# The short convolution's taps as wide GpSimd instructions, and its input turned by VectorE

## The chip, the cores and the metric

One core of a Trainium2 chip runs the whole kernel in one launch. The metric is device time in microseconds (us). The engines are TensorE (PE in the profile, its weight loads PEld), VectorE (DVE), ScalarE (ACT), GpSimd (POOL) and SyncE (SP, which here only issues DMAs).

## What is computed

A decoder trunk of two layers on 256 tokens of 1024 channels, float32. Each layer is a half-weight SwiGLU, a mixer with three branches (gated short convolution, mLSTM, top-k sparse attention) merged by sigmoid gates, a second half-weight SwiGLU, and a gated input embedding; a last RMSNorm follows. The change touches one branch of the mixer:

```python
def short_conv_mixer(b_gate, c_gate, xc, conv_w, w_out):
    u = c_gate * xc                                   # (256, 512)
    up = jnp.pad(u, ((0, 0), (CONV_W - 1, 0), (0, 0)))  # CONV_W = 3
    y = up[:, 0:S] * conv_w[0]
    for j in range(1, CONV_W):
        y = y + up[:, j:j + S] * conv_w[j]
    return (b_gate * y) @ w_out
```

## The kernel before, in words

**Matmuls.** Every product of activations with weights is made of three matmuls (`mm3`, lines 205 to 207): high part by high part, high by low, low by high. A weight comes by DMA into `raw`; ScalarE copies it into the high part `wh` (line 157), VectorE subtracts to get the low part `wl` (line 158: two inputs in SBUF, one output). A *unit* is four blocks of 128 rows by 512 columns: two such pairs of 128x1024. Four units of `wh` and `wl` fit (`wpool`, 4 buffers). `project` (line 222) runs the units of one projection; for each it emits the two splits, then 12 matmuls for each half of the tokens, and after each 12 it calls `tick`.

**Order.** Work that isn't a projection stands in generators in two queues. `tick` takes one step from the head of each queue, so this work is emitted in slices between groups of 12 matmuls; `drain` ticks until a named generator is done. `queues[0]` holds the attention (`dsa`), `queues[1]` in this order the mLSTM gates, the turns of its queries and keys, its heads, then `conv`, `conv_gate`, `mlstm_out(0)`, `mlstm_out(1)`. The emitted order is a priority: a planner that runs when the kernel is built puts each engine's instructions in an order by its own reckoning of when each is ready, and an engine then runs them strictly in that order. So an instruction emitted late can stand early on an engine that would be idle.

**The convolution.** `ccn` (tokens on partitions, 2 x 512 channels) is the product of the gate and the input (lines 756 and 759). `conv` (line 762) turns it so that channels lie on partitions: `pe_turn` (line 289) makes, in two steps of one per half of the tokens, four TensorE transposes of 128x128 into one `tp` tile in PSUM (line 294) and one ScalarE copy to SBUF (line 295). Then, for each of four blocks of 128 channels in a step of its own, VectorE makes the three taps: one tensor-scalar (line 767) and two scalar-tensor-tensor on shifted columns (line 770). `conv_gate` turns the second gate `cbn` on TensorE (line 785), multiplies it into `cv` from PSUM on VectorE (line 786) in two steps, and splits the product into high and low parts.

**What else stands there.** In the same stretch the attention's softmax of the second half of the queries goes: scores on TensorE (line 575), scaling and mask on VectorE (line 577), maximum (line 585), exponentials on ScalarE (line 588), division by the sum on VectorE (line 592), four heads at a time, and then eight transposes of the result into two `tp` tiles on TensorE (line 603). There are two `tp` tiles in all. `mlstm_out` turns the mLSTM output with `turn` (line 283): sixteen VectorE instructions that turn 32x32 blocks, four in a step. Then ScalarE and VectorE scale and split it (lines 804 and 805). The output projections follow: attention, convolution, mLSTM, each behind its gate projection.

Of the kernel before, what the change touches and what calls it, by code (L numbers as in the profile page):

```python
# [13 lines left out]
ALU = mybir.AluOpType  # L14
AX = mybir.AxisListType

P = 128
T = 256
# [19 lines left out]
def trunk_kernel(  # L38
# [7 lines left out]
    nc = tc.nc  # L46
# [11 lines left out]
    def nm(s):  # L58
        uid[0] += 1
        return f"{s}_{uid[0]}"  # L60
# [4 lines left out]
    def tps(shape=(P, 4, P)):  # L65
        return psum.tile(list(shape), F32, name=nm("tp"), tag="tp", bufs=2)
# [11 lines left out]
    def mid(shape, dt=F32):  # L78
        return spool.tile(list(shape), dt, name=nm("mid"), tag="mid", bufs=7)
# [32 lines left out]
    G_FFN1, G_MIX, G_FFN2, G_PLE, G_ML, G_CONV = 0, 16, 32, 48, 64, 80  # L112
    gains = cpool.tile([P, 104], F32, name="gains")
# [165 lines left out]
    def turn(dst, src):  # L279

        for i in range(4):
            for j in range(4):
                nc.vector.transpose(  # L283
                    dst[32 * j:32 * j + 32].rearrange("p f (b i t) -> p b f i t", b=NB, i=4)[:, :, :, i, :],
                    src[32 * i:32 * i + 32].rearrange("p b (f j a) -> p b f j a", j=4, a=32)[:, :, :, j, :])
            if i < 3:
                yield

    def pe_turn(dst, src):

        for b in range(NB):
            tp = tps()
            for f in range(4):
                nc.tensor.transpose(tp[:, f, :], src[:, b, f * P:(f + 1) * P], ident)  # L294
            nc.scalar.activation(dst[:, :, b * P:(b + 1) * P], tp, AF.Copy)
            yield
# [176 lines left out]
    def mixer(l, xs, next_norm):  # L473
# [279 lines left out]
        ccn = mid([P, NB, 512])  # L753
# [6 lines left out]
        cv = mid([P, 4, T])  # L760

        def conv():
            uT = mid([P, 4, T])
            yield from pe_turn(uT, ccn)
            for j in range(4):
                g = [gains[:, G_CONV + 12 * l + 4 * i + j:G_CONV + 12 * l + 4 * i + j + 1] for i in range(3)]
                nc.vector.tensor_scalar(cv[:, j, :], uT[:, j, :], g[2], None, op0=ALU.mult)
                for i in (1, 0):
                    s = 2 - i
                    nc.vector.scalar_tensor_tensor(cv[:, j, s:], uT[:, j, :T - s], g[i], cv[:, j, s:],  # L770
                                                   op0=ALU.mult, op1=ALU.add)
                yield

        queues[1].append(conv())
        cbn = mid([P, NB, 512])
        ps = proj(0)
# [276 lines left out]
```

## Time and profile before

| | |
|---|---|
| median of three runs | 1363.99 us (1363.87 to 1364.86) |
| the profiled execution's own time | 1362.95 us |
| span of its trace | 1361.2 us |
| PE busy | 1350.5 us (99%) |
| DVE busy | 1100.4 us (81%) |
| ACT busy | 727.3 us (53%) |
| POOL busy | 24.9 us (2%) |
| granted TensorE clock, mean | 0.999 |

The span is that of the instructions; the time also holds what lies around them (1.75 us here). Busy matmuls are pipelined: a matmul of 512 columns is shown with 390 ns, while the next one starts some 230 ns after it. In rows of the timeline, columns are start, duration (of the whole row, where several are merged), engine, line, operation, output and inputs, shape, count, and in brackets the idle time before it with what ended it.

### The profile page before, as it was taken

How to read it: one execution, taken by the hardware profiler on the slowest of the kernel's cores; microseconds unless marked ns; L12 is line 12 of the kernel's file. 1: busy time of each engine (PE TensorE's matmuls, PEld its weight loads, DVE VectorE, ACT ScalarE, POOL GpSimd, SP SyncE). 2: the span in 40 equal slices, each digit the busy share in tenths (PEclk: the TensorE clock that was granted, in tenths of full speed). 3: DMA queues.
4: the chain of work that ended last, by engine and by line, in shares of the span. 5: the costliest groups of instructions: out<-in, count | busy, mean ns of one | idle time of the engine just before them, and what ended most of it. 6: DMA issues, size and time to landing. Idle time of an engine off the chain costs nothing.

```text
span 1361.2 us, 17307 instructions
## 1 busy us (share of the span) xinstructions
PE 1350.5 (99%) x6156; PEld 1108.9 (81%) x6156; DVE 1100.4 (81%) x2067; ACT 727.3 (53%) x1137; POOL 24.9 (2%) x42
## 2 busy tenths in 40 slices
PE   9999999999999999999999999999999999999997
PEld 7888888877888888888888888888778888888886
DVE  7988879859957888897788888797697588988976
ACT  6544466666544554454664444666665446444554
POOL 0000000000000000000000000000000000000000
PEclk9999999999999999999999999999999999999999
DMA  7755556643665656476546666655437655565661
GB/s 246 252 199 186 186 179 196 191 124 124 202 204 173 197 191 204 135 249 201 171 155 201 193 203 200 187 180 177 124 118 241 198 168 177 182 196 183 218 203 43
DMA packets 163426, 250.33 MB, mean 184 GB/s; under 512 B 7964, under 2 KB 101260, under 8 KB 163340
## 3 DMA queue, kind: packets, MB, share of 16 engines
q1 hardware_dynamic: 162700, 247.91, 56.9%
q8 instruction: 48, 0.79, 0.2%
q0 software_dynamic: 352, 1.06, 0.2%
q14 instruction: 38, 0.31, 0.1%
q10 hardware_dynamic: 288, 0.26, 0.1%
HBM read 248.14 MB, written 1.06 MB: 183 GB/s over the span
## 4 chain that ended last, share of the span: by engine, by line
PE 95%; DVE 2%; issue 1%; ACT 1%; DMA 0%; SPq 0%; POOLq 0%; POOL 0%; ACTq 0%
PE acc L205 24%; PE acc L207 24%; PE acc L206 24%; PE acc L434 18%; PE tp L264 1%; DVE mid L283 1%; DVE wl L158 1%; PE acc L724 1%; PE acc L575 1%; PE acc L511 0%; PE tp L294 0%; PE tp L603 0%; DMA x<-in_x_dram 0%; PE acc L707 0%; PE acc L537 0%
## 5 line engine op out<-in xcount | busy, mean ns | idle before, releaser
L158 DVE TENSOR_TENSOR wl<-raw,wh 128x1024 fp32r<-128x1024 f32 (+1 forms) x472 | 554.2, 1209 | 95.0 <-ACT wh L157 93.1
L157 ACT ACTIVATE wh<-raw 128x1024 fp32r<-128x1024 f32 (+1 forms) x472 | 475.6, 1044 | 229.1 <-issue 92.5
L205 PE MATMUL acc<-wh,xh 128*128 128x512 f32 (+1 forms) x1384 | 543.4, 393 | 0.8 <-ACT wh L157 0.8
L206 PE MATMUL acc<-wl,xh 128*128 128x512 f32 (+1 forms) x1384 | 537.5, 389 | 0.8 <-DVE wl L158 0.8
L207 PE MATMUL acc<-wh,xl 128*128 128x512 f32 (+1 forms) x1384 | 537.5, 389 | 0.0
L207 PEld LDWEIGHTS acc<-wh,xl 128*128 128x128 f32 x1384 | 260.0, 188 | 53.0
L205 PEld LDWEIGHTS acc<-wh,xh 128*128 128x128 f32 x1384 | 260.2, 188 | 52.6 <-ACT wh L157 1.2
L206 PEld LDWEIGHTS acc<-wl,xh 128*128 128x128 f32 x1384 | 260.3, 188 | 52.2 <-DVE wl L158 1.2
L283 DVE STREAM_TRANSPOSE half<-half 32x128 f32<-32x128 f32 x672 | 203.6, 303 | 12.7 <-DMA half<-in_p_dram 2.7
L434 PE MATMUL acc<-wh,mid 128*128 128x512 f32 x704 | 198.4, 392 | 0.0
L434 PEld LDWEIGHTS acc<-wh,mid 128*128 128x128 f32 x704 | 131.2, 188 | 27.5 <-ACT mid L267 0.9
L434 PE MATMUL acc<-wl,mid 128*128 128x512 f32 x352 | 108.6, 390 | 0.0
L157 ACT ACTIVATE mid<-half 128x512 fp32r<-128x512 f32 x42 | 26.6, 633 | 145.9 <-DVE half L283 145.9
L381 DVE SCALAR_TENSOR_TENSOR half<-acc,r,half 128x256 f32<-128x256 f32 x88 | 41.8, 480 | 64.8 <-ACT half L380 64.8
L380 ACT ACTIVATE half<-acc,r 128x256 f32<-128x256 f32 x88 | 41.2, 472 | 95.7 <-PE acc L207 95.6
L434 PEld LDWEIGHTS acc<-wl,mid 128*128 128x128 f32 x352 | 66.1, 188 | 13.8
L206 PE MATMUL acc<-wl,big 128*128 128x512 f32 x128 | 50.0, 391 | 0.0
L205 PE MATMUL acc<-wh,big 128*128 128x512 f32 x128 | 49.9, 390 | 0.0
L207 PE MATMUL acc<-wh,big 128*128 128x512 f32 x128 | 49.8, 389 | 0.0
L274 ACT ACTIVATE xh<-tp,gains 128x128 fp32r<-128x128 f32 x120 | 39.3, 362 | 12.4 <-DVE xl L275 8.6
L275 DVE SCALAR_TENSOR_TENSOR xl<-tp,gains,xh 128x128 fp32r<-128x128 f32 x120 | 38.3, 345 | 7.5 <-ACT xh L274 6.6
L283 DVE STREAM_TRANSPOSE mid<-big 32x256 f32<-32x256 f32 x96 | 41.8, 436 | 1.3
(189 smaller groups left out, 732.5 us busy)
## 6 DMA issues: line engine op xcount, KB each, us to landing
raw<-in_ffn_w_gu_dram SPq DMA_DIRECT2D x172, 512.0 KB, 5.1
raw<-in_w_in_dram SPq DMA_DIRECT2D x128, 512.0 KB, 4.3
raw<-in_ffn_w_down_dram SPq DMA_DIRECT2D x88, 512.0 KB, 4.7
raw<-in_mlstm_w_out_dram SPq DMA_DIRECT2D x16, 512.0 KB, 3.9
raw<-in_w_o_dram SPq DMA_DIRECT2D x16, 512.0 KB, 4.1
raw<-in_ple_w_gate_dram SPq DMA_DIRECT2D x16, 512.0 KB, 4.9
raw<-in_attn_w_out_dram SPq DMA_DIRECT2D x8, 512.0 KB, 3.9
raw<-in_conv_w_out_dram SPq DMA_DIRECT2D x8, 512.0 KB, 4.8
```

What stands on the lines that cost most here:

```text
L157: made = nc.scalar.activation(hi, v, AF.Copy).ins
L158: nc.vector.tensor_tensor(lo, v, hi.bitcast(F32), op=ALU.subtract)
L205: nc.tensor.matmul(ps, ah, wh, start=start, stop=False)
L206: nc.tensor.matmul(ps, ah, wl, start=False, stop=False)
L207: nc.tensor.matmul(ps, al, wh, start=False, stop=stop)
L264: turned[0] = nc.tensor.transpose(tp[:, j, :], src_of(k0 + j), ident).ins
L274: his.append(nc.scalar.activation(hi, tp[:, j:j + 1, :], AF.Copy, scale=g).ins)
L275: nc.vector.scalar_tensor_tensor(lo, tp[:, j:j + 1, :], g, hi.bitcast(F32), op0=ALU.mult, op1=ALU.subtract)
L283: nc.vector.transpose(dst[32 * j:32 * j + 32].rearrange("p f (b i t) -> p b f i t", b=NB, i=4)[:, :, :, i, :], src[32 * i:32 * i + 32].rea ...
L380: nc.scalar.activation(s[:, b, :], ps[b][:, :FCH], AF.Silu, scale=r)
L381: nc.vector.scalar_tensor_tensor(s[:, b, :], ps[b][:, FCH:], r, s[:, b, :], op0=ALU.mult, op1=ALU.mult)
L434: nc.tensor.matmul(dn[b][n], a, w[:, n * 512:(n + 1) * 512], start=c == 0 and f == 0 and a is ah and w is wh, stop=c == NFC - 1 and f == 1 ...
```

## The change

`conv` turns its input with `turn` (sixteen VectorE instructions in four steps) and makes the taps as five GpSimd instructions over all 4 x 256 columns: three products with a per-channel gain spread along the tokens, two additions of a shifted product. The two products that are added need a tile each (`mid`, a ring of seven buffers). The generator has five steps; before it had six.

```diff
         def conv():
             uT = mid([P, 4, T])
-            yield from pe_turn(uT, ccn)
-            for j in range(4):
-                g = [gains[:, G_CONV + 12 * l + 4 * i + j:G_CONV + 12 * l + 4 * i + j + 1] for i in range(3)]
-                nc.vector.tensor_scalar(cv[:, j, :], uT[:, j, :], g[2], None, op0=ALU.mult)
-                for i in (1, 0):
-                    s = 2 - i
-                    nc.vector.scalar_tensor_tensor(cv[:, j, s:], uT[:, j, :T - s], g[i], cv[:, j, s:],
-                                                   op0=ALU.mult, op1=ALU.add)
-                yield
+            yield from turn(uT, ccn)
+            yield
+            g = [gains[:, G_CONV + 12 * l + 4 * i:G_CONV + 12 * l + 4 * i + 4, None].to_broadcast([P, 4, T])
+                 for i in range(3)]
+            nc.gpsimd.tensor_tensor(cv, uT, g[2], op=ALU.mult)
+            for i in (1, 0):
+                s = 2 - i
+                part = mid([P, 4, T])
+                nc.gpsimd.tensor_tensor(part, uT, g[i], op=ALU.mult)
+                nc.gpsimd.tensor_tensor(cv[:, :, s:], part[:, :, :T - s], cv[:, :, s:], op=ALU.add)
+            yield
```

## Rows read from the trace of the kernel before

**Rows 1.** The page: busy time of each engine, and the chain of work that ended last, by engine.
```profile
PE 1350.5 (99%) x6156; PEld 1108.9 (81%) x6156; DVE 1100.4 (81%) x2067; ACT 727.3 (53%) x1137; POOL 24.9 (2%) x42
...
PE 95%; DVE 2%; issue 1%; ACT 1%; DMA 0%; SPq 0%; POOLq 0%; POOL 0%; ACTq 0%
```

**Rows 2.** The waits of TensorE in the whole span: who waited for whom, us in total, times, longest.
```profile
PE acc L205 <- ACT wh L157: 0.8, 1, 0.8
PE acc L206 <- DVE wl L158: 0.8, 1, 0.8
```

**Rows 3.** Busy time of the engines in two stretches of the second layer (us from the span's start): stretch and its length, then PE, PEld, DVE, ACT, POOL with counts, granted clock, DMA share, GB/s.
```profile
967.20:985.00 17.80, 17.80 (x88) 13.16 (x87) 10.76 (x19) 11.11 (x28) 1.67 (x1) 1.00 0.39 119
985.00:999.00 14.00, 14.00 (x68) 11.17 (x66) 13.74 (x29) 10.01 (x19) 0.00 (x0) 1.00 0.25 71
```

**Rows 4.** The timeline of TensorE around one of the convolution's groups of four transposes, second layer.
```profile
977.58 0.39 PE L207 MATMUL acc<-wh,xl 128*128 128x512 f32 x1
977.90 1.14 PE L575 MATMUL acc<-akT,mid 64*128 64x256 f32 x8
978.97 0.66 PE L294 MATMUL tp<-ident,mid 128*128 128x128 f32 x4
979.38 0.48 PE L205 MATMUL acc<-wh,xh 128*128 128x512 f32 x1
```

**Rows 5.** Groups of instructions by line and shape over the whole span (count, then busy us and mean ns of one). Of line 294 and line 295 a third is the convolution's; the rest turns the mLSTM's queries and keys.
```profile
L283 DVE STREAM_TRANSPOSE mid<-big 32x256 f32<-32x256 f32 x96 | 41.8, 436 | 1.3
...
L294 PE MATMUL tp<-ident,mid 128*128 128x128 f32 x48 | 7.4, 277 | 0.0
L295 ACT ACTIVATE mid<-tp 128x512 f32<-128x512 f32 x12 | 7.0, 586 | 4.7 <-PE tp L294 4.7
...
L770 DVE SCALAR_TENSOR_TENSOR mid<-mid,gains,mid 128x255 f32<-128x255 f32 x8 | 3.8, 478 | 0.0
...
L767 DVE TENSOR_SCALAR mid<-mid,gains 128x256 f32<-128x256 f32 x8 | 2.8, 350 | 0.0
```

**Rows 6.** The timeline of VectorE, second layer: softmax, taps and the first split behind them.
```profile
985.42 1.13 DVE L592 TENSOR_SCALAR big<-big,sm 128x256 f32<-128x256 f32 x4
...
986.73 1.22 DVE L585 TENSOR_REDUCE mx<-big 128x4 f32<-128x1024 f32 x1
...
988.32 0.35 DVE L767 TENSOR_SCALAR mid<-mid,gains 128x256 f32<-128x256 f32 x1
...
989.37 0.35 DVE L767 TENSOR_SCALAR mid<-mid,gains 128x256 f32<-128x256 f32 x1
...
991.15 1.13 DVE L592 TENSOR_SCALAR big<-big,sm 128x256 f32<-128x256 f32 x4
...
992.59 1.21 DVE L158 TENSOR_TENSOR wl<-raw,wh 128x1024 fp32r<-128x1024 f32 x1
```

**Rows 7.** The timeline of ScalarE in the same stretch: the first of the second four exponentials, and the weight copies behind the last of them.
```profile
988.45 0.51 ACT L588 ACTIVATE big<-big,mx 128x256 f32<-128x256 f32 x1 [1.35 <-DVE mx L586]
...
990.44 1.99 ACT L157 ACTIVATE wh<-raw 128x1024 fp32r<-128x1024 f32 x2
```

**Rows 8.** The timeline of TensorE, second layer: the transposes of the softmax and the products behind them.
```profile
994.80 1.03 PE L603 MATMUL tp<-ident,big 128*128 128x128 f32 x8
998.50 1.08 PE L511 MATMUL acc<-half,avn 128*64 128x512 f32 x4
999.51 1.09 PE L603 MATMUL tp<-ident,big 128*128 128x128 f32 x8
```

**Rows 9.** The timeline of GpSimd: one-input instructions over 256 and over 128 columns (the last three are of one shape).
```profile
1.48 0.41 POOL L146 TENSOR_SCALAR_AFFINE_SELECT causT<-causT 128x256 f32<-128x256 f32 x1
...
245.50 1.41 POOL L548 TENSOR_SCALAR_AFFINE_SELECT score<-score 128x128 f32<-128x128 f32 x1 [6.82 <-DVE score L546]
248.73 0.29 POOL L562 TENSOR_SCALAR_AFFINE_SELECT score<-score 128x128 f32<-128x128 f32 x1 [1.82 <-DVE score L560]
258.09 1.16 POOL L562 TENSOR_SCALAR_AFFINE_SELECT score<-score 128x128 f32<-128x128 f32 x1 [9.06 <-DVE score L560]
```

**Rows 10.** The timeline of VectorE beside two of these.
```profile
245.55 1.21 DVE L158 TENSOR_TENSOR wl<-raw,wh 128x1024 fp32r<-128x1024 f32 x1
...
257.87 2.45 DVE L158 TENSOR_TENSOR wl<-raw,wh 128x1024 fp32r<-128x1024 f32 x2
```

**Rows 11.** The timeline of VectorE, second layer, where the output projections begin.
```profile
1018.34 3.57 DVE L283 STREAM_TRANSPOSE mid<-big 32x256 f32<-32x256 f32 x8
1021.94 2.36 DVE L158 TENSOR_TENSOR wl<-raw,wh 128x1024 fp32r<-128x1024 f32 x2
1024.33 3.59 DVE L283 STREAM_TRANSPOSE mid<-big 32x256 f32<-32x256 f32 x8
1027.95 1.22 DVE L158 TENSOR_TENSOR wl<-raw,wh 128x1024 fp32r<-128x1024 f32 x1
```

**Rows 12.** The timeline of TensorE: the first matmuls that use the low parts which VectorE made at 1021.94 and at 1027.95 us.
```profile
1027.29 0.39 PE L206 MATMUL acc<-wl,xh 128*128 128x512 f32 x1
...
1032.73 0.39 PE L206 MATMUL acc<-wl,xh 128*128 128x512 f32 x1
```

**Rows 13.** The timeline of VectorE, second layer: the last write of the convolution's input, and the first product of the gate from PSUM into the taps' result.
```profile
966.42 0.75 DVE L759 SCALAR_TENSOR_TENSOR mid<-acc,r,mid 128x512 f32<-128x512 f32 x1 [3.24 <-PE acc L207]
...
1002.19 0.64 DVE L786 TENSOR_TENSOR mid<-tp,mid 128x512 f32<-128x512 f32 x1
```

## The prediction

> **What bounds the kernel now.** I read the page first: TensorE is busy for 99% of the span and is 95% of the chain that ended last [rows 1]. Then its waits: the two that a weight caused are 0.8 us each in the whole span [rows 2]. So nothing gets faster unless TensorE has less to do, and anything that makes TensorE wait is paid in full. Next I looked at what stands close behind it. In the stretch of the taps, 985 to 999 us, VectorE is busy 13.74 of 14.00 us; in the stretch before it, 967 to 985, only 10.76 of 17.80 [rows 3]. [...] The last view is how long before its use each low part of a weight is ready. It is 4.1 us where VectorE made it at 1021.94 to 1023.16 and TensorE uses it at 1027.29, and 3.6 us for the next, ready at 1029.17 and used at 1032.73 [rows 11, 12]. These are the shortest I found in this mixer. So the margin before TensorE waits is a few us of VectorE time, once per layer.
>
> **What the change takes from TensorE.** Per layer two groups of four transposes (line 294), four groups in all. One runs from 978.97 to the next matmul at 979.38: 0.41 us [rows 4]. The switch into such work (977.58 to 977.90, 0.09 more than between plain matmuls) and the longer first matmul after it (0.48 for 0.39) stay, since line 575 stands in the same slot. Four times 0.41 is **1.64 us**; if the switch went too, 4 x 0.59 = 2.4 us. That is the whole gain there is, 0.12% of the time. ScalarE loses four copies of 0.586 us [rows 5]; it is 53% busy and nothing waits for it here, so I cost that at nothing.
>
> **What it does to VectorE.** Away per layer: twelve taps. One block of three takes from 988.32 to 989.37, 1.05 us [rows 6], so 4.2 us for four. New: sixteen turns of 32x256 at 0.446 each (3.57 for eight, [rows 11]), 7.1 us. Net +2.9 us per layer. But the turns need only `ccn`, which is ready at 967.17 [rows 13], and the 7.04 us that VectorE is idle from 967.2 to 985 [rows 3] hold nearly all of them, if the planner pulls them forward as it does the later turns. I take this: `uT` ready at about 985, and the hole where the taps stood free.
>
> **What it puts on GpSimd.** Five instructions over 1024 columns per layer, four of them with two SBUF inputs that differ in every column, the gains' one spread. No row has one. The nearest: one input, 256 columns 0.41 us, 128 columns 0.29 [rows 9], so 0.94 ns a column and 0.17 fixed. Lower end, the two inputs cost as one: 0.17 + 1024 x 0.94 ns = 1.13 us. Upper end, two reads and a write one after another: 0.17 + 3 x 0.96 = 3.06 us. I take two reads in turn, 0.17 + 2 x 0.96 = **2.1 us**, the middle; five are 10.5 us (5.6 to 15.3). [...] The five are a chain on one engine; behind them in GpSimd's queue stands nothing before the norm that follows the mixer. No DMA moves.
>
> **What they do to each other.** GpSimd's 128-column instruction takes 0.29 us where VectorE runs other work, but 1.41 and 1.16 us where VectorE has just begun a split, and ends only when that split does [rows 9, 10]. The other way round, the pair of splits at 257.87 took 2.45 us against 2.36 for a pair without GpSimd beside it [rows 10, 11]: the second was held by the 0.1 us of GpSimd's that was left. So each waits for the end of the other's instruction; a held VectorE instruction lost 0.1 us only because so little of GpSimd's was left. I take it that a long one holds VectorE to its end. No row shows a division (line 592, one input in SBUF) beside GpSimd: held like a split it costs what follows, not held next to nothing (rival 1). I take held, since at 0.28 us for 256 columns it moves data faster than the two-input tap (0.478, [rows 5]), so it may well use what GpSimd wants. [...]
>
> **The path that this hits** first is the softmax: line 592 (four of 0.28 us), 585, 588, 592 again, then the transposes of line 603 on TensorE at 994.80 [rows 6, 7, 8]. Before, the last division ends at 992.28, 2.5 us early. With GpSimd from 984.85 on and 2.1 us each, VectorE getting in two short divisions between two of GpSimd's: first GpSimd to 986.95, two divisions to 987.5; second to 989.6, two to 990.2; maximum (one input, not held) to 991.4; exponentials, 2.0 us by [rows 7], to 993.7. Third GpSimd to 992.3; a waiting split slips in to 993.45; fourth GpSimd to 995.55; two divisions to 996.1; fifth to 998.2; the last two to 998.75. TensorE, in order, stands before line 603 from about 994.7 to 998.8: **4.1 us per layer**. At 1.13 us each the same count ends at about 994.0, no stall; at 3.06 each it ends near 1003.6, 8.9 us. After the stall VectorE is late by what TensorE is late plus under 1 us, and `conv` has one step less, so four turns (1.8 us) of the mLSTM output come ahead of the splits of [rows 11]; 3.6 us of margin cover both. The two new `mid` tiles take buffers that the mLSTM's queries and keys have left by then (its heads stand ahead of `conv` in the queue), which costs nothing. The branch's product comes behind the attention's, after 1032.73 [rows 12], so the result's own lateness is covered.
>
> **Sum.** Changes are reckoned on the profiled execution (1362.95 us, span 1361.2) and put on the median, 1.04 above it: 1363.99 - 1.64 + 2 x 4.1 = **1370.5 us**.
>
> **Rivals.**
> 1. *Nothing waits* (the other side). GpSimd's instructions are short, or VectorE is held by no more than the 0.1 us seen, or they fall beside the turns. Then only the transposes' time is left: 1363.99 - 1.64 = 1362.35 us, no change that can be told. It decides below some 1.2 us per GpSimd instruction. For it: the 2.5 us of margin before line 603 and the free hole of the taps; and that no held division is on record. Chance 0.27.
> 2. *The taps come late and VectorE waits for them.* If the turns stay where the taps were, GpSimd starts at about 990.4; five of 2.1 with a split of 1.15 between each end at 1005.5. Line 786, at 1002.19 before [rows 13], waits, with the splits behind it, and holds one of the two `tp` tiles that line 603 wants at 999.51 [rows 8]: TensorE waits to about 1006.2, 6.7 us per layer, 1375.7 us. Against it: the planner may put line 786 later. Chance 0.15.
> 3. *VectorE becomes the bound by its own load.* No holding, but the turns aren't pulled forward: +2.9 us, the step that comes earlier +1.8, TensorE 0.8 earlier, less 3.6 of margin [rows 11, 12]: 1.9 us per layer, 1363.99 - 1.64 + 3.8 = 1366.2 us. Chance 0.13.
>
> **How the numbers follow.** My forecast has 0.40; 0.05 is left for an order of the planner's that also clears other TensorE time. A measurement of this kernel can tell 0.2%, 2.7 us: below 1361.3 or above 1366.7. *Faster* is 0.05, since even with the switch 2.4 us is all there is. *Same* is rival 1, the low end of the forecast (0.05) and half of rival 3: 0.38. *Slower* is the rest, 0.57. The range goes from rival 1 less some noise, 1361.8, to the forecast at the upper price, 1363.99 - 1.64 + 17.8 = 1380.1; it holds rivals 2 and 3. The forecast's own range is 1366 to 1380.
>
> **What would show it.** Right: sixteen turns `mid<-mid` per layer lie mostly before 985, five GpSimd rows of about 2 us follow, line 592's rows get longer or stand apart, and TensorE shows a wait for `big` of line 592 before line 603, a few us in each layer. Wrong: GpSimd rows of 1 us, no wait on TensorE, a span some 1.6 us shorter (rival 1); waits of line 603 for a `tp` tile or of line 786 for GpSimd (rival 2); waits of line 206 for line 158 near 1030 us (rival 3). Were the splits stretched beside GpSimd by less than a GpSimd instruction, the holding would be a sharing, and the forecast wrong in its main term.

## The result and the profile after

The changed kernel takes **1370.79 us** (median of five runs, 1368.93 to 1373.35), the kernel before beside it 1363.87: a ratio of 1.0051 [1.0041, 1.0062], 6.9 us more. The forecast was 1370.5. Its profiled execution took 1371.97 us (span 1370.2). The page, its first line as in [rows 1]:

```profile
PE 1354.8 (99%) x6140; PEld 1109.4 (81%) x6140; DVE 1111.0 (81%) x2075; ACT 724.8 (53%) x1133; POOL 45.8 (3%) x52
```

Sixteen TensorE instructions fewer, and yet PE is busy 4.3 us longer: a first hint at the clock. The waits of TensorE name the place, against [rows 2]:

```profile
PE tp L603 <- DVE big L592: 3.8, 4, 1.7
...
PE acc L206 <- DVE wl L158: 0.8, 1, 0.8
```

The first line is new; the wait for a low part is the one of before, so TensorE waits for no split that it didn't wait for then. TensorE around that wait in the second layer, where [rows 8] has 994.80 to 995.59 for the same eight transposes:

```profile
999.43 0.38 PE L603 MATMUL tp<-ident,big 128*128 128x128 f32 x2
1001.53 0.33 PE L603 MATMUL tp<-ident,big 128*128 128x128 f32 x1 [1.71 <-DVE big L592]
1002.05 0.95 PE L603 MATMUL tp<-ident,big 128*128 128x128 f32 x5 [0.20 <-DVE big L592]
1002.65 0.78 PE L205 MATMUL acc<-wh,xh 128*128 128x512 f32 x1
...
1004.22 1.12 PE L787 MATMUL tp<-ident,mid 128*128 128x128 f32 x4
...
1014.19 0.50 PE L205 MATMUL acc<-wh,xh 128*128 128x512 f32 x1
```

The eight take 3.22 us (999.43 to 1002.65) instead of 0.79: a **wait of 2.43 us**. It does not end there: a weight matmul behind it is shown with 0.78 us instead of 0.39. The busy time of the engines by stretch (columns as in [rows 3]):

```profile
999.40:1002.50 3.10, 1.19 (x8) 0.73 (x7) 3.06 (x8) 3.10 (x8) 0.00 (x0) 1.00 0.48 125
1002.50:1005.91 3.41, 3.41 (x12) 2.55 (x11) 3.41 (x4) 3.39 (x5) 0.00 (x0) 0.50 0.83 252
```

For 3.41 us, from the end of the wait on, the granted clock is 0.50, then 1.00 again. The first layer shows the same from 326.66 us on. Count the work that both kernels do here, two groups of line 603, two of line 511, the gate's two groups of transposes and 24 weight matmuls: 10.41 us before (994.80 to 1005.21), 14.76 after (999.43 to 1014.19). The matmul at the end of the same work in the kernel before:

```profile
1005.21 0.48 PE L205 MATMUL acc<-wh,xh 128*128 128x512 f32 x1
```

That is 4.35 us more: 2.43 of wait, and 1.92 behind it. Against it stands TensorE's saving: from the last write of `ccn` to line 603 it takes 28.38 us before [rows 8, 13] and 27.58 after (971.85 to 999.43), 0.80 less. So the sum is 2 x 4.35 less 1.64, 7.1 us; measured 6.9. (This execution has one such drop more, at 22.87 us; it is above the median.)

VectorE, second layer, to be held against [rows 6, 13]:

```profile
971.85 0.75 DVE L759 SCALAR_TENSOR_TENSOR mid<-acc,r,mid 128x512 f32<-128x512 f32 x1 [3.24 <-PE acc L207]
972.64 6.28 DVE L283 STREAM_TRANSPOSE mid<-mid 32x256 f32<-32x256 f32 x14
...
985.23 1.22 DVE L158 TENSOR_TENSOR wl<-raw,wh 128x1024 fp32r<-128x1024 f32 x1
988.02 1.86 DVE L746 TENSOR_TENSOR den<-den,ssq 128x8 f32<-128x8 f32 x1 [1.57 <-POOL ssq L745]
...
992.49 1.11 DVE L586 TENSOR_SCALAR mx<-mx 128x4 f32<-128x4 f32 x1
...
997.52 1.14 DVE L592 TENSOR_SCALAR big<-big,sm 128x256 f32<-128x256 f32 x4
...
1001.12 1.14 DVE L592 TENSOR_SCALAR big<-big,sm 128x256 f32<-128x256 f32 x4
```

And GpSimd:

```profile
985.48 2.51 POOL L745 TENSOR_TENSOR ssq<-ssq,mhalf 128x8 f32<-128x8 f32 x1 [47.78 <-DVE ssq L743]
987.97 1.88 POOL L768 TENSOR_TENSOR mid<-mid,gains 128x1024 f32<-128x1024 f32 x1
989.83 3.74 POOL L772 TENSOR_TENSOR mid<-mid,gains 128x1024 f32<-128x1024 f32 x2
993.53 4.07 POOL L773 TENSOR_TENSOR mid<-mid,mid 128x1020 f32<-128x1020 f32 x2
```

In the kernel before, one of VectorE's idle pieces in this stretch and the end of the short chain, then the chain's step on GpSimd:

```profile
969.42 1.23 DVE L158 TENSOR_TENSOR wl<-raw,wh 128x1024 fp32r<-128x1024 f32 x1 [0.69 <-ACT wh L157]
...
976.82 0.17 DVE L746 TENSOR_TENSOR den<-den,ssq 128x8 f32<-128x8 f32 x1 [1.85 <-POOL ssq L745]
```

```profile
975.12 1.67 POOL L745 TENSOR_TENSOR ssq<-ssq,mhalf 128x8 f32<-128x8 f32 x1 [42.98 <-DVE ssq L743]
```

Three things are to be seen. The turns run as one block of fourteen as soon as `ccn` is there, and two splits that became ready while the block ran (ScalarE had written their `wh` by 972.91 and 974.83) come behind it. Two tiny instructions (lines 746 and 586, 0.17 us each in the kernel before) last 1.86 and 1.11 us and end just when a GpSimd instruction does (989.85 and 993.57). And the divisions of line 592 are *not* held: four take 1.14 us, as in [rows 6]; GpSimd has just ended.

The lateness of the second group of divisions can be counted from the last write of `ccn`. Line 746 comes 16.17 us behind it (before: 10.40), so it is **5.77 late before GpSimd's taps begin**. Lines 746 and 586 lose **1.69 + 0.94 = 2.63** to GpSimd. Against that, the taps (4.2 us) that used to stand between line 746 and the last division are gone. The last division ends 30.41 us behind `ccn` instead of 25.86: 4.55 late in all, and the 2.5 us of margin, less the 0.8 that TensorE comes earlier, take only 1.7 of it. The wait is a little shorter than the 2.85 that are left, since only the last of the eight transposes needs the last division.

### The profile page after: what moved, and what is told of

The parts are those of the page before. It is cut to its first block, busy times and chain, and to the rows that moved or that the text cites. A ratio compares the mean times of both kernels' runs of the same rounds, so it can differ in the third digit from the quotient of the medians.

```text
span 1370.2 us, 17286 instructions
## 1 busy us (share of the span) xinstructions
PE 1354.8 (99%) x6140; PEld 1109.4 (81%) x6140; DVE 1111.0 (81%) x2075; ACT 724.8 (53%) x1133; POOL 45.8 (3%) x52
## 4 chain that ended last, share of the span: by engine, by line
PE 93%; DVE 4%; ACT 1%; issue 1%; POOL 0%; POOLq 0%; ACTq 0%
PE acc L205 24%; PE acc L206 24%; PE acc L207 24%; PE acc L434 18%; PE tp L264 1%; DVE wl L158 1%; DVE mid L283 1%; PE acc L724 1%; PE acc L511 0%; ACT wh L157 0%; PE acc L575 0%; PE tp L603 0%; PE acc L707 0%; ACT big L588 0%; PE tp L294 0%
## 5 line engine op out<-in xcount | busy, mean ns | idle before, releaser
L308 POOL TENSOR_TENSOR r<-ms,mhalf 128x1 f32<-128x1 f32 x16 | 10.3, 645 | 1086.3 <-ACT xh L274 560.4
```

## The experiments

Theory 1: GpSimd holds VectorE (the forecast's). Theory 2: the planner's order of the turns alone makes the softmax late. Theory 3: what is lost beyond the wait is the clock. Each kernel was timed against the kernel before on the same chip (medians 1363.64 to 1363.96 us).

| kernel | median us | ratio to before |
|---|---|---|
| turn_only | 1366.44 | 1.0020 [1.0011, 1.0029] |
| taps_only | 1373.83 | 1.0076 [1.0063, 1.0088] |
| write_only | 1367.97 | 1.0031 [1.0020, 1.0043] |
| keep_warm | 1378.56 | 1.0110 [1.0097, 1.0124] |
| keep_warm3 | 1374.09 | 1.0075 [1.0062, 1.0088] |
| behind_both | 1389.12 | 1.0182 [1.0168, 1.0196] |
| late_conv | 1371.82 | 1.0057 [1.0044, 1.0071] |
| turn_spread | 1368.82 | 1.0037 [1.0023, 1.0051] |
| spread_taps | 1384.55 | 1.0151 [1.0138, 1.0165] |

**The turn alone** (the kernel before with `turn` for `pe_turn`, taps on VectorE in one step).

```diff
-            yield from pe_turn(uT, ccn)
+            yield from turn(uT, ccn)
+            yield
```

> The input is turned by VectorE as in the changed kernel, but the taps stay on VectorE (twelve instructions, in the step where GpSimd's five stood). No GpSimd work, so nothing is held. Theory 1 (GpSimd's holding of VectorE makes the softmax late): no wait of TensorE before line 603, and the four groups of transposes saved: 1363.9 - 1.6 = 1362.2 us. Theory 2 (the sixteen turns, which VectorE runs as one block of 6.3 us ahead of splits that are ready, and ahead of the mLSTM's small chain, make the softmax late by themselves, and the taps come on top): the last division ends about as late as in the changed kernel, TensorE waits 2 us or more per layer before line 603, time 1367 to 1372 us.

It took 2.7 us more than before. The waits of TensorE, then VectorE:

```profile
PE tp L603 <- DVE big L592: 2.9, 4, 1.3
```

```profile
968.12 0.75 DVE L759 SCALAR_TENSOR_TENSOR mid<-acc,r,mid 128x512 f32<-128x512 f32 x1 [3.24 <-PE acc L207]
968.91 6.27 DVE L283 STREAM_TRANSPOSE mid<-mid 32x256 f32<-32x256 f32 x14
...
984.28 0.17 DVE L746 TENSOR_TENSOR den<-den,ssq 128x8 f32<-128x8 f32 x1 [1.57 <-POOL ssq L745]
...
996.93 1.13 DVE L592 TENSOR_SCALAR big<-big,sm 128x256 f32<-128x256 f32 x4
```

Nothing is held here, and line 746 is as late as in the changed kernel (16.16 us behind the last write of `ccn`). TensorE waits 1.88 us per layer (eight transposes in 2.67), at a full clock throughout. The order alone, with VectorE's own taps in the softmax, is enough for a wait, though a little less came than theory 2 had expected (2 us or more, 1367 to 1372).

**The taps alone** (TensorE's turn kept, taps on GpSimd, six steps).

```diff
-            yield from turn(uT, ccn)
-            yield
+            yield from pe_turn(uT, ccn)
```

> The taps are GpSimd's five, but the input is turned by TensorE as before; the number of steps is that of before, so VectorE's order is that of before without the taps. GpSimd works from about 986 us (second layer) on for 9.5 us, beside the second half of the softmax. Theory 1 (holding): a tensor-scalar of 128x4 (line 586), the splits or the divisions are held 1 to 2 us each time, the last division comes 3 to 5 us late against a margin of 2.5, TensorE waits 1 to 3 us per layer: 1366 to 1370 us. Theory 2 (order): the 4.2 us of taps that are gone outweigh the holding; no wait before line 603, 1363.9 us within 0.7.

VectorE's order is now that of before without the taps, and the holding stands alone:

```profile
990.93 1.79 DVE L158 TENSOR_TENSOR wl<-raw,wh 128x1024 fp32r<-128x1024 f32 x1
992.65 1.86 DVE L586 TENSOR_SCALAR mx<-mx 128x4 f32<-128x4 f32 x1
...
996.87 5.00 DVE L592 TENSOR_SCALAR big<-big,sm 128x256 f32<-128x256 f32 x4
```

```profile
PE tp L603 <- DVE big L592: 6.1, 2, 3.0
```

A split takes 1.79 for 1.21, line 586 1.86 for 0.17, four divisions 5.00 for 1.13 [rows 6]. The eight transposes take 4.04 us in the first layer and 4.52 in the second, waits of 3.3 and 3.7. This is the mechanism of the forecast near its price (4.1), in a kernel that lacks the other half of the change. The time lies above the expected 1366 to 1370: alone, this half costs 10.1 us, more than the whole change with 6.9. TensorE's saving is missing here, and GpSimd starts at 989.56, so the divisions fall beside it. So theory 1 holds, and either half by itself makes TensorE wait at line 603.

**GpSimd work that reads next to nothing** (the taps are left out; a short copy and nine fills stand in their place).

```diff
-            nc.gpsimd.tensor_tensor(cv, uT, g[2], op=ALU.mult)
+            nc.gpsimd.tensor_copy(cv[:, :, 0:1], uT[:, :, 0:1])
+            for _ in range(9):
+                nc.gpsimd.memset(cv, 0.5)
...
-                part = mid([P, 4, T])
-                nc.gpsimd.tensor_tensor(part, uT, g[i], op=ALU.mult)
-                nc.gpsimd.tensor_tensor(cv[:, :, s:], part[:, :, :T - s], cv[:, :, s:], op=ALU.add)
```

> The changed kernel with the five tap instructions replaced by GpSimd work that reads next to nothing: a copy of four columns and nine constant fills of 1024 columns (the taps' arithmetic is left out). VectorE's order is the changed kernel's. [...] Theory 2 (the order alone makes the wait): no held lines, yet 1.9 us of wait per layer as in the kernel with the turn alone, 1366.4.

VectorE, then GpSimd:

```profile
985.44 0.17 DVE L746 TENSOR_TENSOR den<-den,ssq 128x8 f32<-128x8 f32 x1 [1.57 <-POOL ssq L745]
...
988.22 0.40 DVE L586 TENSOR_SCALAR mx<-mx 128x4 f32<-128x4 f32 x1
...
992.54 2.68 DVE L592 TENSOR_SCALAR big<-big,sm 128x256 f32<-128x256 f32 x4
```

```profile
985.38 0.18 POOL L768 COPY mid<-mid 128x4 f32<-128x4 f32 x1
985.62 9.20 POOL L770 MEMSET mid<- 128x1024 f32 x9
```

Theory 1 stood here in the form that GpSimd's reading is what holds VectorE; then lines 746 and 586 take 0.17 us and the kernel 1362 to 1366. If any work of GpSimd's holds it, they take 1.1 to 1.9 us and the kernel about 1370. The time was 2 us above the first range (1368.0), because that form was wrong: the first four divisions, one input each, last 2.68 us beside fills that read nothing, for 1.13 in the kernel before [rows 6] and 1.14 for the second four here, when the fills had ended. Reading wasn't needed for that. What a fill does to an instruction with two inputs stays open: line 746 met the short copy here and not a fill, so its 0.17 us says only that without long GpSimd work before it it wasn't held. Line 746 comes 16.16 us behind `ccn` here too, so the order's part is still there; TensorE's wait is 1.49 us (transposes 2.28), and the clock stays at 1.00.

**Work in TensorE's wait** (nine, then three matmuls on zeros ahead of the second softmax's transposes, in the changed kernel).

```diff
+                    if b == 1 and sb == 0:
+                        wp = acc()
+                        for _ in range(9):
+                            nc.tensor.matmul(wp, warm, x[0][:, :512], start=True, stop=True)
```

> The changed kernel with nine matmuls of 128x512 on zeros (their result is not used) right before the transposes of line 603 of the second half, so that TensorE works while it would wait. Nine take about 2.3 us, as long as the wait of 2.3 to 2.4 us. Theory 3 (after the wait TensorE gets the lower clock for 3.4 us, and half of that, some 2 us per layer, is lost): no drop of the granted clock, the matmuls behind line 603 start 0.23 us apart again, time 4 us less than the changed kernel, 1366.5 to 1367 us. If the clock costs nothing beyond the wait: the same time as the changed kernel, 1370.8 us, or some us more where the nine are not covered.

> Repeat with the size mended: one of those matmuls took 0.86 us, so nine were 7.7 us and far more than the wait of 2.4 us. Now three, about 2.57 us per layer, ahead of the second softmax's transposes. Theory 3 (the clock after the wait costs about 2 us per layer): the work fits into the wait, the clock stays at 1.00, about 1367 us, some 4 less than the changed kernel; no drop but the one at the end. If the clock after the wait cost nothing: the changed kernel's 1370.8 us.

Nine were mis-sized: they took 7.72 us per layer, and the kernel 7.8 us more than the changed one, in place of the expected 4 less. That is 10.6 us of work beyond the two waits of 2.43, less 2.8. The 2.8 are found behind the nine. The same work as counted above takes 10.98 us there, with no wait and the clock at 1.00 (line 607 is line 603 of the changed kernel):

```profile
1009.01 1.04 PE L607 MATMUL tp<-ident,big 128*128 128x128 f32 x8
...
1019.99 0.50 PE L205 MATMUL acc<-wh,xh 128*128 128x512 f32 x1
```

That is 0.57 more than before in place of 1.92: the sum behind the wait shrinks where the clock stays up and the tiles have time. With three, the time (1374.09 for an expected 1367) can't tell: their 2.57 us fill the wait, but the planner now puts the gate's transposes behind one weight matmul instead of three, and they wait 1.88 us for a `tp` tile that ScalarE empties (line 609) behind four weight copies (3.88 us). Within this kernel, however, one layer has the drop and the other hasn't, with the same instructions. The stretches of the two layers, with the granted clock and TensorE's matmuls in 3.41 us (9 and 18):

```profile
329.42:332.83 3.41, 3.41 (x9) 2.65 (x9) 3.14 (x7) 2.09 (x3) 0.00 (x0) 0.50 0.95 293
1007.00:1010.41 3.41, 3.41 (x18) 2.17 (x16) 3.18 (x7) 2.57 (x4) 0.00 (x0) 1.00 0.95 305
```

Eleven weight matmuls take 4.29 us in the first layer (328.93 to 333.22) and 2.72 in the second (1007.00 to 1009.73). **A drop of 3.41 us cost 1.6 us** where TensorE had only work. Theory 3 holds for that. In the changed kernel the drop overlaps another wait, so its own part is smaller (below).

**All of `conv` behind the softmax**, by two ways: three quarters of the turns behind line 746 and the last behind the last division (behind_both); all turns behind the last division, `conv` four steps later and the gate's product with it (late_conv).

```diff
-            yield from turn(uT, ccn)
-            yield
+            for i in range(4):
+                with tc.issue_after(marks['den'] if i < 3 else marks['div']):
...
+                yield
```

`marks` keeps line 746 and the last division as they are emitted, and `issue_after` sets what it encloses behind that instruction on VectorE. late_conv has `marks['div']` for all four portions, and four `yield` ahead of them.

> The changed kernel with the first twelve turns ordered behind the mLSTM's last small instruction (line 746 of the changed kernel) and the last four behind the last division of the softmax. So GpSimd's taps can only begin when the softmax is over: nothing of it is held, and the mLSTM's chain comes in time. The twelve turns (5.4 us) stand ahead of the softmax. Theory 1 (holding): no wait before line 603, 1362 to 1363 us. Theory 2 (order): the softmax starts some 4 us later than before, less the taps' 4.2 us that are gone from it; the wait is about 1 us per layer or less, and with little drop of the clock 1363 to 1366 us. A wait of line 788 for GpSimd, or of TensorE for a tp tile, could come in its place, since the taps end later: then 1366 us or more.

> The changed kernel with conv started four steps later in the queue and its sixteen turns placed behind the second softmax's last division, so that GpSimd works only after the softmax. The gate's product comes later too. If all that the change costs is the softmax's lateness (theories 1 and 2 together): no wait before line 603, no drop of the clock, and TensorE's 1.64 us come through: about 1362.2 us. If GpSimd beside the splits of the mLSTM's output and of the projections costs as much there: waits of weight matmuls near 1030 us, 1364 to 1370.

In behind_both TensorE waits somewhere else:

```profile
PE tp L606 <- DVE mid L796: 18.0, 2, 9.0
```

```profile
1024.47 0.69 DVE L796 TENSOR_TENSOR mid<-tp,mid 128x512 f32<-128x512 f32 x1 [5.80 <-POOL mid L781]
```

The gate's product (line 796 here) waits for GpSimd's last addition with a `tp` tile in hand, and the softmax's transposes stand before that tile for 9 us. That is rival 2, at 9.0 us per layer for the 6.7 reckoned, and 1389.12 us for the hoped-for 1362 to 1366. With the gate later too (late_conv) no wait of line 603 is left, and the last division ends 24.29 us behind `ccn`, earlier than in the kernel before. But now other waits come, and VectorE beside GpSimd shows why:

```profile
PE acc L206 <- DVE wl L158: 6.5, 7, 2.4
```

```profile
1002.26 6.90 DVE L158 TENSOR_TENSOR wl<-raw,wh 128x1024 fp32r<-128x1024 f32 x3
1009.08 6.78 DVE L829 SCALAR_TENSOR_TENSOR big<-big,den,half 128x256 f32<-128x256 f32 x4
```

```profile
1002.30 2.93 POOL L778 TENSOR_TENSOR mid<-mid,gains 128x1024 f32<-128x1024 f32 x1 [21.08 <-DVE mid L772]
1005.20 5.70 POOL L782 TENSOR_TENSOR mid<-mid,gains 128x1024 f32<-128x1024 f32 x2
1010.87 4.32 POOL L783 TENSOR_TENSOR mid<-mid,mid 128x1020 f32<-128x1020 f32 x2
```

Three splits take 6.90 us (3.49 in the changed kernel), four scalings of the mLSTM output 6.78 (1.67), and GpSimd's five 12.95 instead of 9.7. VectorE loses 8.5 us in a stretch with 3.6 us of margin [rows 11, 12], and the splits behind are late. My 1362.2 failed (1371.82): the waits named here are 6.5 of the 9.8 us that were lost with TensorE's 1.64 counted in, and the rest isn't taken apart. The holding came here too, with GpSimd's work in its new place, and from 985 to 1035 us VectorE was busy 49.0 of 50 us before.

**The turns spread over VectorE's idle stretches**, with the taps on VectorE (turn_spread) and on GpSimd (spread_taps).

```diff
+            for i, key in enumerate([None, 'den', ('max', 1, 0), ('div', 1, 0)]):
+                with ExitStack() as behind:
+                    if key in marks:
+                        behind.enter_context(tc.issue_after(marks[key]))
...
+                yield
```

The keys stand for line 743, and for line 586 and the last division of the first four heads in the second half of the queries.

> Turns on VectorE, taps left on VectorE as before; the turns go in four portions into the stretches where VectorE was idle (at once; behind line 743; behind the first maximum of the second softmax; behind its first divisions) and no longer as one block. If the kernel with the turn alone was late only by the order (theory 2): no wait before line 603, no longer L745 (1.67 us), and TensorE's 1.64 us come through: about 1362.1 us. If VectorE's own load of 2.9 us more per layer is what counts: weight matmuls wait near 1030 us and 1364 to 1367.

> The same order of the turns, taps on GpSimd. GpSimd now starts behind the first divisions, so lines 746 and 586 are free of it, and the second divisions and the splits beside them are not. Theory 1: four divisions take about 5 us instead of 1.14 and the splits between 1.8 and 2.4 instead of 1.21, TensorE waits about 3 us before line 603 in each layer: 1368 to 1373 us. Theory 2 (the order was all): 1362.

turn_spread has no wait of line 603 for a division. It has these instead, and lost 4.9 us:

```profile
PE acc L206 <- DVE wl L158: 3.0, 3, 1.2
PE tp L606 <- DVE mid L797: 2.7, 2, 1.3
```

That is above the expected 1362.1 and also above 1364 to 1367. The 2.9 us per layer more on VectorE come out at the splits, as in rival 3, and at the gate's product. The load alone doesn't set this price: turn_only has the same turns and taps, lost 2.7 us, and TensorE waits there for a division but for neither of these. Here the taps begin 25.70 us behind `ccn` and there 16.97, so they stand ahead of the gate's product and the splits. Load and placing are not parted by these two. spread_taps is the clearest case of the holding. The divisions take 1.13 us for four in turn_spread. Here they are in the view of their tile (count, ns of one as least, median and most), then in VectorE's timeline, then GpSimd beside them:

```profile
L594 DVE TENSOR_SCALAR big<-big,sm x4: 1976/2030/2144, 1005.4 to 1011.2; 128x256 f32<-128x256 f32 x4
```

```profile
1005.39 7.94 DVE L594 TENSOR_SCALAR big<-big,sm 128x256 f32<-128x256 f32 x4
```

```profile
1001.46 2.93 POOL L778 TENSOR_TENSOR mid<-mid,gains 128x1024 f32<-128x1024 f32 x1 [14.14 <-DVE mid L772]
1004.36 4.76 POOL L782 TENSOR_TENSOR mid<-mid,gains 128x1024 f32<-128x1024 f32 x2
1009.09 4.11 POOL L783 TENSOR_TENSOR mid<-mid,mid 128x1020 f32<-128x1020 f32 x2
```

Each division waits for the end of one GpSimd instruction, **one division per GpSimd instruction**, so four last 7.94 us, to 1013.33; GpSimd ends at 1013.20. TensorE waits 8.2 us per layer (eight transposes in 9.00, from 1004.52 to 1013.52). The clock falls within the wait and stays low for 10.24 us, about half of them behind it:

```profile
1008.47:1018.71 10.24, 6.43 (x19) 5.04 (x20) 10.24 (x11) 4.69 (x6) 4.64 (x3) 0.50 0.26 95
```

So 1384.55 us, against an expected 1368 to 1373 that counted 5 us for the four.

No kernel beat the one before. What there is to gain, 1.64 us, is about as much as the intervals above leave open (1.2 to 1.9 us either way), and each way of taking it lost more than that.

## Why the prediction was right, and where it wasn't

*TensorE sets the time, and any wait is paid in full*: right. The cost came as waits of TensorE and what followed them, 4.35 us in each layer.

*1.64 us less on TensorE*: right, 0.80 per layer measured. The switch into such work stayed, as said.

*7.1 us of turns, pulled forward into VectorE's idle time*: sixteen take 7.2 us, and they ran early, from 972.64 on; `uT` was ready sooner than forecast (981.5, which is 976.1 on the clock of the kernel before, for 985). The conclusion from it, that this costs nothing, is **the first step that failed**. The idle time was in pieces, between splits that waited for ScalarE; the turns took it in one block, and the splits, then the short chain of lines 739 to 746, came behind. That chain goes through GpSimd (line 745), which lost another 0.84 us beside a split (2.51 for 1.67). So the softmax started 5.77 us late. The trace of before had the pieces: the sum of idle time alone hid them.

*2.1 us per GpSimd instruction*: right, 1.88 for a product and 2.0 for an addition where VectorE leaves it alone; up to 2.93 beside a split. Two of the five, the additions, have two inputs that differ in every column, not four; the three products have the gain spread.

*VectorE is held to the end of the GpSimd instruction, divisions included*: right as a mechanism (taps_only 5.00 us, spread_taps 7.94 us for four divisions, write_only 2.68), wrong in where it falls in this kernel. **The second step that failed** is the placing: since the softmax was late, GpSimd was done when the first division came, and lines 746 and 586 were held in place of divisions, for 2.63 us. Two divisions between two GpSimd instructions, as the count had it, is also wrong: it is one.

*A wait before line 603 of 4.1 us*: right in its place, too large. It was 2.43. **What the forecast left out** makes up for that: 1.92 us per layer behind the wait. Of these 0.8 are the clock (the gate's four transposes 0.77 for 0.41, nine weight matmuls 2.68 for 2.23; in write_only, at the full clock, the same take 0.41 and 2.25). Another 0.8 are three weight matmuls that take 1.57 instead of 0.78. In write_only, at a full clock, they take 1.65, because line 787 there waits for the `tp` tile that ScalarE empties behind three weight copies; so in the changed kernel half clock and this wait lie on top of each other, and I can't part them. The last 0.3 is one more switch between transposes and weight matmuls, since the gate's transposes stand elsewhere. Two errors of opposite sign, 4.1 for 2.43 and nothing for 1.92, made a sum that is nearly exact. That closeness is luck: the forecast's number was better than its reasons.

*The splits of [rows 11] aren't hit*: right; the wait for `wl` is 0.8 us once, as before.

*The rivals.* Rival 1 (nothing waits) is out: GpSimd's instructions last 1.88 us and more, and hold VectorE. Rival 2 (the gate's product waits for GpSimd and holds a `tp` tile) didn't come here because the turns were early; behind_both is what it looks like. Rival 3 (VectorE's own load) can be seen where GpSimd has no taps: 2.7 us in turn_only and 4.9 in turn_spread, more than the 2.2 reckoned, but both hold the placing of the turns and taps as well.

## What to carry to other kernels

Work given to GpSimd was not simply taken from VectorE in these runs: while a long GpSimd instruction ran, VectorE's products (line 746, 1.86 us for 0.17), differences (three splits, 6.90 for 3.49 in late_conv) and scalings (line 586, 1.11 for 0.17; four divisions, 7.94 for 1.13 in spread_taps) between SBUF and SBUF waited for its end one by one, tiny ones and one-input ones too; maxima (1.22) and reciprocals (0.18) did not. So look in the trace for 0.17 us instructions that last as long as the other engine's. Idle time is no cover as a sum: ask which pieces it is in, what becomes ready in it, and what short chain stands behind a block put there. And behind a wait of TensorE of some us reckon with its clock as well as with the wait: 2.43 us of wait came here with 3.41 at 0.50.

## What the runs showed of the hardware

- **Held one at a time.** Of four short divisions, each got through at the end of a different GpSimd instruction (spread_taps, 1.98 to 2.14 us each, for 0.35 in the changed kernel). Beside GpSimd's taps in the changed kernel the maximum (line 585), the scaling out of PSUM (line 577) and the reciprocal (line 590) kept their times: 1.22 us, 1.29 for two, 0.18.
- **Fills hold too.** GpSimd fills of 1024 columns (nine in 9.20 us), which read nothing, held one-input divisions (write_only, four in 2.68 us, for 1.14 when the fills had ended).
- **Both lose.** A GpSimd product lasts 1.88 us in the changed kernel and 2.93 beside splits in late_conv.
- **The clock around a wait.** In the changed kernel's profile a wait of 2.4 us came with 3.41 us at 0.50 in both layers. Waits of 1.5 and 1.9 us (write_only, turn_only) came with none, but one of 1.88 us (keep_warm3) with 3.41 us in the first layer and none in the second. In taps_only TensorE stood still for 3.0 us in each layer, in the first with no drop and in the second with 6.83 us; in spread_taps a wait of 8.2 came with 10.24. In the last two the low clock began before the wait ended (at 1000.70, with TensorE idle to 1001.66, and at 1008.47, with the wait to 1013.52). So it isn't fixed by the length of the wait alone. The runs of the changed kernel differ with it: mean granted clock 0.999 at 1368.93 us, 0.995 at 1371.97 and 1373.35.
